# Cosine attention on one core: ten buffers for V in place of six, pair 3's squares in halves, and new engine orders

## The chip, the core and the metric

The kernel runs on one core of a Trainium2 chip. The metric is the device time of one execution in microseconds (us). The engines of the core work side by side, each through its own list of instructions in order: TensorE (PE in the profile), VectorE (DVE), ScalarE (ACT), GpSimd (POOL), and SyncE (SP), which here only issues DMA transfers. An instruction that waits for another engine holds up everything behind it on its own engine.

## The reference

Inputs Q, K, V are float32 of shape 8 x 12 x 512 x 64 (batch, heads, sequence, width), tau is 0.1. The core of it:

```python
Q_norm = Q / (np.linalg.norm(Q, axis=-1, keepdims=True) + 1e-10)
K_norm = K / (np.linalg.norm(K, axis=-1, keepdims=True) + 1e-10)
scores = np.einsum('bhqd,bhkd->bhqk', Q_norm, K_norm) / tau
weights = np.exp(scores - np.max(scores, axis=-1, keepdims=True))
weights = weights / (np.sum(weights, axis=-1, keepdims=True) + 1e-10)
return np.einsum('bhqk,bhkd->bhqd', weights, V).astype(np.float32)
```

## The kernel before, in words

The 96 heads are worked on as 48 pairs, s = 0 to 47. A pair goes through these steps, which the text names by their keys in the code:

- LD(s,0), LD(s,1), LV(s): SyncE loads Q, K and V of the pair, 256 KB each (L299, L302). For pair 0 the loads are in halves, K's on ScalarE's queue (L296).
- SQ(s): squares of Q and K, on GpSimd as one instruction (L325); for the pairs in `SQ_ON` in parts, on ScalarE or GpSimd (L317, L319); for pair 0 L227 and L229.
- SSQ(s,1), RED(s,w): sums of squares over the width. For K (and for the first pairs Q as well) TensorE adds eight slices (L342) and DVE reduces the rest (L349); otherwise DVE reduces alone (L353).
- NEW(g,k): the reciprocal norms of a group g of one to four pairs, by Newton steps on DVE (L377 to L386); for the first four pairs by a logarithm and an exponential on ScalarE, LOG(g) at L367 and NEW(g,7) at L370.
- SCL(s,w): Q and K times the reciprocal norms (L404), Q's on DVE, K's mostly on GpSimd.
- TR(s,w): TensorE transposes both (L410; pair 0 L254, L256), and EVA(s) copies the result out on DVE (L417; pair 0 L267).
- SCO(s,c): for each of four blocks c of keys, two score products on TensorE (L446), and EXP(s,c) on ScalarE (L469): exp of scores over tau for both heads, 128 x 1024. For pair 0 the first two blocks come by head, in halves of 128 x 512.
- VC(s): GpSimd copies V to bfloat16 (L474), beside a column of ones that is set once (L180).
- PV(s,h,i): the products with V on TensorE (L486), which give the sum of weights in a 65th column; RCP and NRM on DVE divide by it (L497, L499), and ST(s) stores the pair from SyncE (L503). The last pair is done in three pieces (L460, L514, L525, L527).

The scores are cosines over 0.1 and need no maximum subtracted.

Nothing is scheduled at run time: `ORDER` holds, for each engine, the numbers of the operations in the order in which they are issued. Waits are derived from what each operation needs. TensorE's list also has filler products (`-256` is one of 256 columns, L188), behind eight warm-up products (L185). Buffers are rings, whose sizes are `RINGS`:

```python
R_QK, R_V, R_SQ, R_QN, R_QT, R_ET, R_O, R_X = RINGS
```

A load into a ring waits until the buffer's last user is done. For V this is

```python
P.add(("LV", s), "sp", "ld", s + VLAG, [key("VC", s - R_V)],
      lambda e: e.dma_start(out=vf[iv][:, :, :], in_=src(V, s)), slot=f"v{iv}")
```

so LV(s) waits for VC(s - 6). SyncE's list from pair 12 on goes ST(s-12), LV(s-3), LD(s,0), LD(s,1), with small shifts.

Of the kernel before, what the change touches and what calls it, by code (L numbers as in the profile page):

```python
# [106 lines left out]
def bass_cosine_similarity_attention_kernel(  # L107
# [20 lines left out]
    qk = [sb(f"qk{i}", [128, 2, 2, NT * DIM], f32) for i in range(R_QK)]  # L128
# [156 lines left out]
    def pair(s):  # L285
# [6 lines left out]
        for w, x in ((0, Q), (1, K)):  # L292
            if s == 0:
                for h in range(2):
                    P.add(("LD", 0, w, h), "act" if w else "sp", "ldh", -1000 + h,  [],
                          lambda e, w=w, x=x, h=h: e.dma_start(out=qk[iq][:, w, h], in_=src(x, s)[:, h]), slot=f"head{w}_{h}")  # L296
                continue
            P.add(("LD", s, w), "sp", "ld1" if s == 1 else "ld", s, [*([("SCL", 0, w, 0), ("SCL", 0, w, 1), ("SQ", 0, w, 0), ("SQ", 0, w, 1)] if s == R_QK else [key("SCL", s - R_QK, w), *(squares(s - R_QK, w) if s >= R_QK else [])])],
                  lambda e, w=w, x=x: e.dma_start(out=qk[iq][:, w], in_=src(x, s)),  # L299
                  slot=f"first{s}_{w}" if s <= 2 else f"qk{iq}")  # L300
# [242 lines left out]
SQ_ON = {1: ("act", ("act", "pool")), 2: ("act", "pool")}  # L543
# [8 lines left out]
RINGS = 18, 6, 6, 3, 3, 3, 8, 3  # L552
# [17 lines left out]
def slack(s, most):  # L570
# [5 lines left out]
        "7 8 64 65 103 104 11 141 142 66 178 179 105 221 222 143 255 256 180 297 298 223 331 332 257 374 375 299 408 "  # L576
        "409 333 450 451 63 376 102 410 140 452 177 220 484 485 526 527 560 561 486 603 604 528 637 638 254 562 679 680 "
        "296 605 713 714 330 639 755 756 373 681 789 790 407 715 832 833 449 757 866 867 483 791 900 901 525 834 934 "
        "935 559 868 977 978 602 902 1011 1012 636 936 1045 1046 678 979 1079 1080 712 1013 1121 1122 754 1047 1155 "
        "1156 788 1081 1189 1190 831 1123 1223 1224 865 1157 1266 1267 899 1191 1300 1301 933 1225 1334 1335 976 1268 "  # L580
        "1368 1369 1010 1302 1411 1412 1044 1336 1445 1446 1078 1370 1479 1480 1120 1413 1513 1514 1154 1447 1555 1556 "
        "1188 1481 1589 1590 1222 1515 1623 1624 1265 1557 1657 1658 1299 1591 1699 1700 1333 1625 1733 1734 1367 1659 "
        "1767 1768 1410 1701 1444 1735 1478 1769 1512 1554 1588 1622 1656 1698 1732 1766 1796 1810 "
    ),
    "pool": (
        "0 1 2 14 27 22 35 69 4 107 50 144 89 181 224 164 127 258 207 300 230 334 377 272 360 306 241 411 283 453 349 "
        "470 394 317 436 487 529 425 459 563 606 640 501 546 535 682 512 716 578 758 792 589 835 654 688 623 869 665 "
        "903 730 699 764 741 775 937 980 807 1014 963 852 818 875 1048 909 1082 886 1124 920 952 986 1158 1020 1192 997 "
        "1226 1269 1141 1107 1031 1303 1096 1065 1175 1252 1209 1130 1337 1164 1371 1198 1320 1414 1354 1448 1241 1286 "
        "1397 1309 1482 1516 1431 1558 1343 1499 1465 1386 1420 1454 1626 1592 1660 1702 1609 1643 1736 1685 1530 1564 "  # L590
        "1598 1541 1719 1632 1575 1770 1753 1789 1674 1708 1742 1776 "
    ),
    "dve": (
        "5 13 15 26 28 19 24 21 32 71 73 37 34 109 78 111 76 80 116 114 148 146 118 151 153 182 155 184 225 227 55 185 "
        "56 186 61 187 62 188 189 94 190 95 192 191 193 194 196 100 261 101 198 259 301 303 228 262 138 263 139 264 232 "
        "265 132 266 133 267 337 268 175 269 270 169 378 170 304 274 176 380 335 212 338 213 339 218 340 219 341 342 "
        "308 343 344 345 246 347 414 247 346 252 381 253 454 351 412 288 456 383 415 294 289 416 295 417 385 418 488 "
        "419 490 420 322 422 421 323 423 328 457 329 427 530 365 532 366 491 371 492 372 493 564 494 461 607 399 495 "
        "566 496 400 498 497 405 499 406 641 503 533 609 441 567 442 568 447 569 448 570 537 571 683 572 643 574 573 "
        "475 575 576 481 476 482 717 610 580 612 685 517 644 759 645 518 646 523 614 647 524 648 793 649 551 651 719 "  # L600
        "650 552 652 557 836 558 656 686 594 761 795 720 595 721 690 722 723 870 724 600 725 838 601 727 726 628 872 "
        "629 728 904 634 635 732 762 906 670 796 671 797 676 798 677 799 766 800 938 801 802 803 805 839 704 940 710 "
        "705 711 804 809 841 981 1015 746 983 747 752 843 753 873 780 1017 781 907 1049 877 786 787 1051 823 941 942 "
        "824 943 1083 944 911 945 829 946 830 948 947 1125 950 1085 857 858 949 863 864 954 1054 984 1159 897 898 891 "
        "1127 892 988 1052 1018 1193 931 925 1161 926 932 1022 1227 1270 1195 968 1086 969 1087 974 1088 975 1089 1090 "
        "1056 1091 1093 1092 1128 1002 1229 1003 1094 1008 1009 1098 1304 1036 1272 1037 1042 1043 1162 1132 1196 1076 "
        "1077 1070 1306 1071 1338 1166 1372 1340 1230 1112 1231 1118 1113 1232 1119 1233 1200 1234 1235 1415 1237 1236 "
        "1238 1239 1146 1152 1374 1153 1147 1275 1273 1243 1341 1180 1417 1181 1307 1186 1187 1277 1449 1214 1451 1215 "
        "1483 1517 1311 1220 1221 1559 1485 1257 1375 1258 1376 1377 1378 1263 1379 1264 1380 1382 1381 1345 1452 1384 "
        "1519 1291 1292 1297 1298 1418 1388 1486 1325 1561 1326 1383 1331 1332 1422 1627 1488 1593 1359 1595 1360 1365 "  # L610
        "1366 1456 1703 1629 1402 1520 1403 1521 1522 1408 1523 1409 1524 1490 1525 1526 1527 1528 1562 1436 1663 1437 "
        "1442 1443 1532 1661 1470 1705 1471 1596 1566 1476 1477 1630 1504 1739 1505 1737 1600 1510 1511 1771 1546 1773 "
        "1547 1664 1665 1666 1667 1668 1552 1669 1553 1671 1670 1634 1672 1580 1706 1581 1586 1587 1740 1676 1774 1614 "
        "1620 1615 1621 1710 1648 1654 1649 1655 1744 1690 1691 1778 1696 1697 1724 1725 1730 1731 1758 1759 1764 1765 "
        "1801 1802 1794 1795 1808 1809 "
    ),
    "pe": (
        "6 -256 -256 -256 -256 -256 -192 23 20 -256 70 36 -256 72 -128 42 33 38 108 39 43 110 46 79 77 48 81 83 147 145 "
        "117 115 85 51 52 57 87 58 53 59 152 119 154 54 183 121 60 226 123 125 90 91 92 93 156 96 97 98 158 99 260 160 "
        "195 197 162 134 135 136 199 137 302 128 201 129 231 130 203 229 131 171 205 172 173 174 336 233 165 166 167 "  # L620
        "168 235 271 237 273 208 209 239 210 211 379 275 214 215 216 277 217 305 307 279 242 243 244 281 245 413 248 "
        "309 249 250 251 311 348 284 285 313 286 287 350 315 290 291 455 352 292 293 354 382 384 356 318 319 324 358 "
        "320 321 489 386 325 326 388 327 361 390 424 426 362 392 363 364 531 428 367 368 369 370 430 460 458 432 395 "
        "396 397 398 434 401 565 462 402 403 404 464 437 438 439 466 500 440 502 468 608 443 444 504 445 446 534 506 "
        "536 471 472 508 473 474 642 510 477 478 538 479 480 540 577 513 514 542 515 519 579 544 520 516 684 581 521 "
        "611 583 522 613 585 547 548 549 587 550 718 553 615 554 555 556 617 794 590 591 619 653 655 621 592 593 760 "
        "657 689 687 659 596 597 598 624 661 599 837 625 663 626 627 871 691 630 631 632 693 666 633 667 695 729 731 "
        "668 697 669 672 905 733 673 674 675 765 735 763 737 700 701 702 739 703 939 706 767 707 708 709 769 806 771 "
        "808 742 773 748 743 744 745 810 749 982 750 812 751 842 840 814 776 777 778 816 779 1016 782 844 783 784 876 "
        "846 874 785 819 820 848 821 822 1050 850 910 908 878 825 826 827 880 853 828 854 882 855 856 884 1084 859 912 "  # L630
        "860 861 862 914 951 953 916 887 888 889 918 893 894 895 890 955 896 1126 957 985 987 959 927 928 929 961 930 "
        "921 922 923 989 924 1160 991 1019 1021 993 964 965 970 995 966 967 1194 1023 971 972 973 1025 1055 1053 1027 "
        "998 999 1004 1029 1000 1001 1228 1057 1005 1006 1007 1059 1097 1032 1033 1061 1095 1034 1035 1063 1038 1271 "
# [60 lines left out]
```

## Time and profile before

| | |
|---|---|
| median of 4 runs | 191.08 us (190.92 to 192.71) |
| the profiled execution: its own time | 192.71 us |
| its span, first to last instruction | 190.7 us |
| busy: ACT, PE, DVE, POOL | 182.7, 177.5, 164.6, 154.9 us |
| moved by DMA | 50.75 MB, 266 GB/s over the span |
| GpSimd waiting for K loads at L325 | 5.8 us, 8 times |
| SyncE waiting at V loads (L302) for V copies (L474) | 23.9 us, 14 times |
| SyncE waiting at stores (L503) for NRM (L499) | 38.6 us, 23 times |

The times are medians over executions; the profile is of one execution, whose own time lies 2.0 us above its span. In profile rows, the first number of a timeline row is the start in us from the span's start, the second the duration; "x4" is a count of merged instructions, and the brackets give the idle time of the engine just before and what ended it. In a row of the groups, the numbers after the first bar are busy us and mean ns of one, after the second bar the idle us before them. Records of ScalarE start before the previous one has ended, so busy time there includes some waiting.

### The profile page before, as it was taken

The numbers are of one execution on the slowest core, as the hardware profiler recorded it, in microseconds if no ns is written. First come the engines' busy times: TensorE is split into PE (matmuls) and PEld (weight loads), VectorE is DVE, ScalarE is ACT, GpSimd is POOL, SyncE is SP. The second block draws the span as 40 slices with busy tenths as digits, with TensorE's granted clock in tenths as the row PEclk, the third lists the DMA queues.
The fourth block names the chain that finished last, engine by engine and source line by source line (L and its number), as shares of the span: only waits on it lengthen the run. The fifth ranks groups of instructions, "written<-read, shape, count | busy, mean of one in ns | idle before, by whom it ended". The sixth has DMA issues, their size and how long they took to land.

```text
span 190.7 us, 6683 instructions
## 1 busy us (share of the span) xinstructions
PE 177.5 (93%) x2729; PEld 110.7 (58%) x2729; DVE 164.6 (86%) x530; ACT 182.7 (96%) x214; POOL 154.9 (81%) x144
## 2 busy tenths in 40 slices
PE   7989899999999999999999999899999999999983
PEld 2636566656665566566566566555656656555552
DVE  2689999999999999999998898999898989885543
ACT  4699999999999999999999999999999999999993
POOL 3689899999999999999996998999798699260000
PEclk9999999999999999999999999999999999999999
DMA  5999996999999989999999299997899775231133
GB/s 157 343 353 349 348 359 206 314 348 373 378 344 284 286 251 311 347 322 311 327 305 335 89 281 321 344 381 257 281 274 315 255 229 155 70 112 55 58 110 110
DMA packets 52445, 50.75 MB, mean 266 GB/s; under 512 B 3136, under 2 KB 52416, under 8 KB 52416
## 3 DMA queue, kind: packets, MB, share of 16 engines
q1 hardware_dynamic: 51984, 50.02, 81.1%
q8 instruction: 21, 0.34, 0.7%
q10 hardware_dynamic: 432, 0.33, 0.5%
q14 instruction: 8, 0.07, 0.1%
HBM read 37.75 MB, written 12.58 MB: 264 GB/s over the span
## 4 chain that ended last, share of the span: by engine, by line
ACT 84%; DMA 6%; POOL 4%; PE 3%; SPq 1%; issue 1%; DVE 1%
ACT et L469 82%; DMA qk<-in_K_dram 3%; DMA qk<-in_Q_dram 3%; POOL sq L325 2%; PE scps L446 1%; POOL qn L404 1%; PE ops L342 1%; POOL vb L474 1%; PE tps L410 1%; PE ops L486 0%; SPq L296 0%; ACT et L460 0%; DVE ob L527 0%; ACT sq L317 0%; SPq L299 0%
## 5 line engine op out<-in xcount | busy, mean ns | idle before, releaser
L469 ACT ACTIVATE et<-scps 128x1024 bf16<-128x1024 f32 (+1 forms) x193 | 176.1, 1202 | 0.6 <-PE scps L446 0.5
L325 POOL TENSOR_TENSOR sq<-qk 128x1024 bf16<-128x1024 f32 x45 | 84.8, 1893 | 5.8 <-DMA qk<-in_K_dram 5.8
L446 PE MATMUL scps<-qt 64*128 64x512 bf16 x384 | 75.6, 386 | 7.0 <-ACT et L469 2.2
L486 PE MATMUL ops<-vb,et 128*128 128x65 bf16 x1504 | 75.9, 195 | 0.4 <-DVE ob L499 0.2
L486 PEld LDWEIGHTS ops<-vb,et 128*128 128x128 bf16 x1504 | 56.5, 98 | 30.5 <-issue 23.3
L404 POOL TENSOR_TENSOR qn<-qk,rk 128x512 bf16<-128x512 f32 x37 | 38.2, 1043 | 4.2 <-DVE rk L382 4.0
L499 DVE TENSOR_TENSOR ob<-ops,rd 128x256 f32<-128x256 f32 x94 | 38.8, 419 | 0.8
L404 DVE TENSOR_TENSOR qn<-qk,nps 128x512 bf16<-128x512 f32 x57 | 37.8, 677 | 0.1
L417 DVE COPY qt<-tps 128x1024 bf16<-128x1024 bf16 x47 | 32.2, 686 | 3.8 <-PE tps L410 3.5
L446 PEld LDWEIGHTS scps<-qt 64*128 64x128 bf16 x384 | 19.3, 93 | 26.0 <-ACT et L469 12.6
L410 PE MATMUL tps<-ident,qn 128*128 128x128 bf16 x376 | 33.5, 221 | 0.9 <-POOL qn L404 0.7
L353 DVE TENSOR_REDUCE nps<-sq 128x8 f32<-128x512 bf16 x44 | 29.9, 684 | 3.0 <-POOL sq L325 2.7
L474 POOL TENSOR_SCALAR vb<-vf 128x512 bf16<-128x512 f32 x48 | 29.4, 626 | 0.8 <-DMA vf<-in_V_dram 0.8
L410 PEld LDWEIGHTS tps<-ident,qn 128*128 128x128 bf16 x376 | 21.5, 98 | 12.2 <-issue 5.6
L497 DVE RECIPROCAL rd<-ops 128x4 f32<-128x4 f32 x94 | 16.3, 176 | 8.5 <-PE ops L486 6.9
L342 PE MATMUL ops<-sq,ident 128*128 128x64 bf16 x400 | 19.8, 194 | 0.3
L342 PEld LDWEIGHTS ops<-sq,ident 128*128 128x128 bf16 x400 | 14.9, 98 | 2.9 <-issue 2.0
L349 DVE TENSOR_REDUCE nps<-ops 128x8 f32<-128x64 f32 x44 | 9.3, 213 | 0.2
L377 DVE TENSOR_TENSOR nps<-nps,ys 128x32 f32<-128x32 f32 (+1 forms) x30 | 6.2, 207 | 0.2
L378 DVE SCALAR_TENSOR_TENSOR nps<-nps,ys 128x32 f32<-128x32 f32 (+1 forms) x30 | 6.2, 208 | 0.1
L185 PE MATMUL ops<-warm_in,ident 128*128 128x512 bf16 x8 | 3.6, 631 | 1.4 <-POOL eps L178 1.4
L382 DVE SCALAR_TENSOR_TENSOR nps<-nps,ys 128x16 f32<-128x16 f32 (+1 forms) x22 | 3.9, 182 | 0.1
(50 smaller groups left out, 41.0 us busy)
## 6 DMA issues: line engine op xcount, KB each, us to landing
vf<-in_V_dram SPq DMA_DIRECT2D x48, 256.0 KB, 5.4
qk<-in_Q_dram SPq DMA_DIRECT2D x47, 256.0 KB, 4.6
qk<-in_K_dram SPq DMA_DIRECT2D x47, 256.0 KB, 5.5
out_dram<-ob SPq DMA_DIRECT2D x47, 256.0 KB, 4.2
qk<-in_Q_dram SPq DMA_DIRECT2D x2, 128.0 KB, 2.7
qk<-in_K_dram ACTq DMA_DIRECT2D x2, 128.0 KB, 2.9
out_dram<-ob SPq DMA_DIRECT2D x1, 128.0 KB, 1.7
out_dram<-ob ACTq DMA_DIRECT2D x1, 64.0 KB, 1.6
```

The source lines that it names most:

```text
L325: lambda e: e.tensor_tensor(out=sqf, in0=data, in1=data, op=ALU.mult))
L342: last = e.matmul(out=o_ps[bank][:, 320:384], lhsT=ident[:, :], rhs=sq[iqs][:, 8 * w : 8 * w + 8, 8 * k : 8 * k + 8], start=(k == 0), stop ...
L353: lambda e, w=w, dst=dst: e.tensor_reduce(out=dst, in_=sq[iqs][:, 8 * w : 8 * w + 8, :], axis=AX.X, op=ALU.add))
L404: lambda e, w=w, r=r: e.tensor_tensor(out=qn[iqn][:, w].rearrange("p t h d -> p h t d"), in0=qk[iq][:, w].rearrange("p h (t d) -> p h t d" ...
L410: last = e.transpose(t_ps[:, w, t, :], qn[iqn][:, w, t].rearrange("p h d -> p (h d)"), ident[:, :])
L417: lambda e: e.tensor_copy(out=qt[iqt][:, :, :, :].rearrange("p w t x -> p (w t x)"), in_=t_ps[:, :, :, :].rearrange("p w t x -> p (w t x)")))
L446: last = e.matmul(out=sc_ps[:, 2 * b + h, :], lhsT=qt[iqt][64 * h : 64 * h + 64, 1, c, :], rhs=qt[iqt][64 * h : 64 * h + 64, 0, :, :], sta ...
L469: lambda e, c=c, b=b, hs=hs: e.activation(out=et[iet][:, c, hs[0] : hs[-1] + 1, :], in_=sc_ps[:, 2 * b + hs[0] : 2 * b + hs[-1] + 1, :], f ...
L474: lambda e: e.tensor_scalar(out=vb[:, iq, :, :, 0:DIM].rearrange("p c h d -> p h c d"), in0=vf[iv][:, :, :].rearrange("p h (c d) -> p h c ...
L486: last = e.matmul(out=o_ps[h][:, 65 * t : 65 * t + 65], lhsT=et[iet][:, c, h, 128 * t : 128 * t + 128], rhs=vb[:, iq, c, h, :], start=(c = ...
L497: lambda e, h=h, grid=grid: e.reciprocal(out=rd[io][:, h, :], in_=grid[:, :, DIM]))
L499: lambda e, h=h, grid=grid: e.tensor_tensor(out=ob[io][:, h], in0=grid[:, :, 0:DIM], in1=rd[io][:, h, :].unsqueeze(2).to_broadcast([128, N ...
```

## The change

`RINGS` gives V ten buffers in place of six. The squares of pair 3 are two GpSimd instructions, one for Q and one for K, in place of one, and its two loads get a semaphore each, so that the first half can start with Q alone. The five orders come from a new search; the numbers above 144 shift by one since pair 3 has one operation more.

```diff
-                  slot=f"first{s}_{w}" if s <= 2 else f"qk{iq}")
+                  slot=f"first{s}_{w}" if s <= 3 else f"qk{iq}")
...
-SQ_ON = {1: ("act", ("act", "pool")), 2: ("act", "pool")}
+SQ_ON = {1: ("act", ("act", "pool")), 2: ("act", "pool"), 3: ("pool", "pool")}
...
-RINGS = 18, 6, 6, 3, 3, 3, 8, 3
+RINGS = 18, 10, 6, 3, 3, 3, 8, 3
```

The orders, read back into keys. SyncE's is the same. ScalarE's differs in the first pairs only:

```
ACT before: ... SQ2.0 LOG1 EXP0.1.0 NEW1 EXP0.0.0 EXP0.0.1 EXP0.1.1 LOG2 EXP0.2 NEW2 EXP0.3 EXP1.0 EXP1.1 LOG3 NEW3 EXP1.2 ...
ACT after:  ... SQ2.0 EXP0.1.0 LOG1 NEW1 EXP0.0.0 EXP0.0.1 EXP0.1.1 LOG2 EXP0.2 NEW2 EXP0.3 EXP1.0 LOG3 EXP1.1 NEW3 EXP1.2 ...
```

TensorE's and GpSimd's starts (f is a filler with its columns; vone is the memset of L180, one, eye and eps are the constants of L174, L175 and L178):

```
PE before: warm f256 x5 f192 TR0.1.0 TR0.0.0 f256 SSQ1.0 TR0.1.1 f256 SSQ1.1 f128 SCO0.1.0 TR0.0.1 SCO0.0.0 SSQ2.0 ...
PE after:  warm f256 x3 f192 TR0.1.0 TR0.0.0 f256 SSQ1.0 TR0.1.1 f128 SCO0.1.0 SSQ1.1 TR0.0.1 SCO0.0.0 SSQ2.0 ...

POOL before: one eye eps SQ0.1.0 SQ0.1.1 SCL0.1.0 SCL0.1.1 SQ1.1.1 vone SQ2.1 VC0 SQ3.0 VC1 SQ4.0 ...
POOL after:  eps one eye vone SQ0.1.0 SQ0.1.1 SCL0.1.0 SCL0.1.1 SQ1.1.1 SQ2.1 VC0 SQ3.0 SQ3.1 VC1 SQ4.0 ...
```

and a stretch of GpSimd's in mid-run:

```
POOL before: ... SQ29 VC23 SCL24.1 SCL25.1 SQ30 SCL26.1 SQ31 VC25 SQ32 SQ33 VC29 VC28 VC26 SQ34 SCL28.1 VC27 VC30 VC32 VC31 SCL29.1 SQ35 SCL30.1 SQ36 SCL31.1 VC34 ...
POOL after:  ... SQ29 VC27 SCL24.1 SQ30 SCL25.1 VC24 SCL26.1 VC28 VC25 VC26 SQ31 SQ32 SQ33 SQ34 SCL28.1 SCL29.1 VC31 SCL30.1 SQ35 VC29 SQ36 VC32 VC34 VC30 SCL31.1 VC33 ...
```

On TensorE and DVE the operations of neighbouring pairs change places throughout.

## The prediction

> **What bounds the kernel now.** I read the page first, then ScalarE's own timeline at the start, then the chain in order of time, and last the queues of GpSimd and SyncE at the place where the chain leaves ScalarE.
>
> ```profile
> span 190.7 us, 6683 instructions
> ...
> PE 177.5 (93%) x2729; PEld 110.7 (58%) x2729; DVE 164.6 (86%) x530; ACT 182.7 (96%) x214; POOL 154.9 (81%) x144
> ...
> ACT 84%; DMA 6%; POOL 4%; PE 3%; SPq 1%; issue 1%; DVE 1%
> ...
> L469 ACT ACTIVATE et<-scps 128x1024 bf16<-128x1024 f32 (+1 forms) x193 | 176.1, 1202 | 0.6 <-PE scps L446 0.5
> L325 POOL TENSOR_TENSOR sq<-qk 128x1024 bf16<-128x1024 f32 x45 | 84.8, 1893 | 5.8 <-DMA qk<-in_K_dram 5.8
> ```
>
> ScalarE's exponentials are the bound: 193 of them, and only 0.6 us of idle before them in the whole run. The 1202 ns is no price, because the records overlap. The chain in order of time gives the price:
>
> ```profile
> 15.87 88.02 ACT et L469 x96
> ...
> 121.11 65.19 ACT et L469 x71
> ```
>
> 96 exponentials in 88.02 us are 0.917 us each, and the 71 later ones, 0.918. Between the two pieces lies a loss that the busy share hides: of 193, 175 are in the chain's other ACT pieces or ahead of it (two halves at 9.21 and 9.79), so 18 lie between. From 103.89 (end of the 96) to 122.13 (end of the first of the 71: 121.11 + 1.02) 19 exponentials end; at 0.917 that is 17.42 us, and it took 18.24. So **0.82 us** is lost in mid-run, and nowhere else after 16 us. The rest of the span is the start (first exponential at 9.21) and the end (last exponential ends at about 187.3, then 3.4 us of products, scaling and stores). Only start, middle and end can give anything.
>
> **The start.** The first exponential, and what stands ahead of it:
>
> ```profile
> 8.15 0.63 ACT L317 ACTIVATE sq<-qk 128x512 bf16<-128x512 f32 x1 [0.24 <-DMA qk<-in_Q_dram]
> 8.99 0.31 ACT L367 ACTIVATE ys<-xs,eps 128x16 f32<-128x16 f32 x1 [0.21 <-DVE xs L349]
> 9.21 0.58 ACT L469 ACTIVATE et<-scps 128x512 bf16<-128x512 f32 x1
> 9.68 0.18 ACT L370 ACTIVATE nps<-ys 128x16 f32<-128x16 f32 x1
> ```
>
> ```profile
> 7.68 0.39 PE L254 MATMUL scps<-ident,qn 128*128 128x128 bf16 x4
> 7.90 0.27 PE L188 MATMUL scps<-warm_in,ident 128*128 128x256 bf16 x1
> 8.30 0.39 PE L342 MATMUL ops<-sq,ident 128*128 128x64 bf16 x8
> 8.53 0.22 PE L188 MATMUL scps<-warm_in,ident 128*128 128x128 bf16 x1
> 8.68 0.39 PE L446 MATMUL scps<-qt 64*128 64x512 bf16 x1
> ```
>
> SSQ(1,1) (8.30) waits for a square of pair 1, made from the K load that lands late; the first score product stands behind it though its own operands (EVA, copied by 7.58) are ready. The new PE order puts the product first, after the 128-column filler: filler from about 8.05, product at about 8.2. On ScalarE the square of pair 2 (8.15 to 8.78) still stands ahead, so the first exponential starts at about 8.7 in place of 9.21: 0.5 us earlier. It then goes back. LOG(1) now comes behind that exponential. SSQ(1,1) follows the product at about 8.5 and RED 0.43 later (8.30 to 8.73 in the rows), done by 9.15; LOG(1) 9.2 to 9.5, NEW(1) 9.53 to 9.73 (9.86 before), the next exponential about 0.15 earlier than before. The scale, transpose and copy of pair 1 (L404, L410, L417) keep their order, hence also about 0.2 earlier. LOG(3) moves ahead of EXP(1,1), and everything on ScalarE queues behind that wait: it needs RED(3,1), behind pair 2's scale products on DVE. The squares of pair 3 in halves start at about 10.6 with Q and end at 12.7 (13.06 before), so RED(3,1) ends at about 14.4 where EXP(1,0) lets ScalarE go at about 14.25: 0.1 us back. Net of the start: **0.1 us gained** (ends: 0.3 lost if LOG(3) waits for a late K, 0.5 gained if nothing comes back).
>
> The split itself: two 128x512 squares at 1.04 (POOL's row of that shape) against one of 1.89 are 0.19 us more on POOL, covered by the 0.59 us it idled before that square. [...] POOL is full from 30 to 100 us, by which the split would cost 0.19; at 11 us the row shows it waiting, so it costs 0. The memset of `vb` (0.74) goes into POOL's 2.2 us wait for the first K load and frees 0.7 us at 8.1, which the K load of pair 2 uses up.
>
> Fewer fillers: three of 256 columns leave, two of them ahead of the first transposes. [...] Without the two fillers (0.21 each) TensorE idles about 0.4 us before 6.16, after some 4.3 us of unbroken work. [...] I take 0 and keep +1.0 for the range.
>
> **The middle.** Why ScalarE lost 0.82 us:
>
> ```profile
> 103.17 0.38 SPq L503 DMA_DIRECT2D out_dram<-ob  x1
> 107.42 0.37 SPq L302 DMA_DIRECT2D vf<-in_V_dram  x1
> 107.83 0.47 SPq L299 DMA_DIRECT2D qk<-in_Q_dram  x1
> 108.35 0.47 SPq L299 DMA_DIRECT2D qk<-in_K_dram  x1
> ```
>
> ```profile
> 117.40 1.89 POOL L325 TENSOR_TENSOR sq<-qk 128x1024 bf16<-128x1024 f32 x1 [0.91 <-DMA qk<-in_K_dram]
> 119.25 1.04 POOL L404 TENSOR_TENSOR qn<-qk,rk 128x512 bf16<-128x512 f32 x1
> ```
>
> SyncE is one queue. At 103.55 it stops at V of pair 32, whose buffer is free only when POOL has copied V of pair 26 (107.40, an old copy placed late), and the Q and K loads behind it wait with it. In all SyncE stands 23.9 us, 14 times, at V loads for these copies. The K loads then come late: POOL idles 5.8 us, and here 0.91 at 117.40; the scale product behind it ends at 120.29, the transpose on PE waits 0.52 for it, the score product stands behind that, and ScalarE starts at 121.11 after 0.45 of shown idle. The two smaller losses (108.5, 111.4) hang on the square at 103.74, which had waited 0.76 for K.
>
> With ten buffers V of pair 32 asks for the copy of pair 22, made long before. SyncE's order is unchanged, so it then stands only at stores (38.6 us for NRM): after the store at 103.17 the loads go at 103.6 to 104.5, **about 4 us earlier**, more than the 0.91 and 0.76 missed. POOL is next to be late only on its own work. So up to 0.82 us goes. The bytes and the count of transfers stay.
>
> **The sum.** Of the profiled run: 190.7 - 0.1 - 0.8 = 189.8 span, and with the 2.0 around it 191.8 against 192.71. But the other three runs are 190.92 to 191.17, 1.6 us under the profiled one, so they cannot hold all of its late loads. I take half of the 0.82: 191.08 - 0.1 - 0.4 = **190.6 us**. The end's order is the same on ScalarE and nearly so on PE: 0. The searched orders of PE, DVE and POOL move hundreds of instructions; by the rows no instruction gets dearer from its neighbours (all 45 whole squares on POOL take 1.89), and PE's longest burst between two score products in mid-run falls or stays, so I cost them at 0 while ScalarE covers them.
>
> **Rivals.**
> *Nothing to gain* (191.1): the unprofiled runs have no mid-run loss and LOG(3) takes the start back. For it: their 1.6 us. Against: the 23.9 us of SyncE are the program's.
> *Everything gained* (189.9): 0.82 in every run and 0.4 at the start. For it: the queue's wait is fixed by POOL's order. Against: under 189.17 it would also need the end.
> *A V load takes the place of the K load, slower* (192.0): POOL's new order puts V copies ahead of scale products, such as V of pair 34 ahead of SCL(31,1), where before it stood behind. That load was issued at 112.85 and V takes 5.4 to land: 118.3, while POOL now arrives at about 117.7. The price is known: 0.91 of waiting cost ScalarE 0.56, so a wait decides from about 0.35 on. Three such places at 0.4 give +1.2 and a slower result. Against: earlier issue by SyncE also serves V.
> [...]
>
> **How the numbers follow.** Forecast (190.2 to 190.9) 0.50, nothing gained 0.20, everything 0.13, slower by waits or clock 0.17. Range 189.4 to 192.2. 1% (1.9 us), about what a measurement of this kernel can tell from no change, is more than all of the start and middle together: faster by it 0.04, taken from the third case's edge. Slower by it needs twice the last rival's price: 0.08. The rest is within.
>
> **What would show it.** Right: no V load waiting on SyncE for POOL in mid-run; POOL's waits for K fall from 5.8 to 2 or less; exponentials of 0.917 without a break after 16 us; first exponential near 8.7, but EXP(1,2) only 0.1 to 0.3 before its 15.80. Wrong: POOL waiting for V, DVE or PE waiting for POOL's scale products with a break on ScalarE, or 128-column transposes still at 0.107 us pitch after 7.5 us.

## The result, and the profile after

The changed kernel takes 191.14 us (median of 43 runs, 190.56 to 194.56). The kernel before, run beside it, takes 191.87 us (64 runs, 190.76 to 195.74). The ratio is 0.9964 [0.9952, 0.9976]; of 191.87 that is 0.69 us less [0.46, 0.92]. Medians and quartiles here are of all runs, while the ratios leave out the slow ones, such as 3 of these 43 (193.65 to 194.56, at a mean granted TensorE clock of 0.977 to 0.986), so a ratio is not exactly the quotient of two medians. The gain is not a plain shift: the lower quartile goes from 191.33 to 190.95, the upper from 192.53 to 191.43. So the lower edge of the times moves by 0.4 us and the upper by 1.1.

The profiled execution took 190.94 us and its span is 188.9. The page of the profile, at the rows that were shown of before:

```profile
span 188.9 us, 6679 instructions
...
PE 176.4 (93%) x2726; PEld 110.3 (58%) x2726; DVE 164.9 (87%) x530; ACT 182.2 (96%) x214; POOL 154.8 (82%) x145
...
ACT 94%; DMA 3%; SPq 1%; issue 1%; DVE 1%; PE 0%
...
L469 ACT ACTIVATE et<-scps 128x1024 bf16<-128x1024 f32 (+1 forms) x193 | 175.8, 1243 | 0.0
L325 POOL TENSOR_TENSOR sq<-qk 128x1024 bf16<-128x1024 f32 x44 | 82.8, 1893 | 3.0 <-DMA qk<-in_K_dram 2.9
```

The chain is on ScalarE for 94% of the span instead of 84%; POOL, 4% before, is gone from it, and PE's share falls from 3% to 0. The chain in order of time (start, length, what) says this most sharply:

```profile
14.93 169.58 ACT et L469 x185
```

From 14.93 us to 184.51 ScalarE runs 185 exponentials without a break, 0.917 each. The 169.57 us are a ruler for all that follows: in the eight other kernels below whose trace has no break, the same 185 take 169.54 to 169.59 us. Such a kernel differs from another almost only by when the 185 begin.

ScalarE's timeline at the start:

```profile
7.48 0.63 ACT L317 ACTIVATE sq<-qk 128x512 bf16<-128x512 f32 x1 [0.31 <-DMA qk<-in_Q_dram]
8.04 0.60 ACT L469 ACTIVATE et<-scps 128x512 bf16<-128x512 f32 x1
8.64 0.31 ACT L367 ACTIVATE ys<-xs,eps 128x16 f32<-128x16 f32 x1
8.98 0.19 ACT L370 ACTIVATE nps<-ys 128x16 f32<-128x16 f32 x1
9.10 1.56 ACT L469 ACTIVATE et<-scps 128x512 bf16<-128x512 f32 x3
...
13.63 0.31 ACT L367 ACTIVATE ys<-xs,eps 128x16 f32<-128x16 f32 x1
13.85 1.00 ACT L469 ACTIVATE et<-scps 128x1024 bf16<-128x1024 f32 x1
14.75 0.18 ACT L370 ACTIVATE nps<-ys 128x16 f32<-128x16 f32 x1
14.86 3.75 ACT L469 ACTIVATE et<-scps 128x1024 bf16<-128x1024 f32 x4
```

and, of before, the rows up to EXP(1,2):

```profile
15.33 0.32 ACT L367 ACTIVATE ys<-xs,eps 128x16 f32<-128x16 f32 x1
15.68 0.19 ACT L370 ACTIVATE nps<-ys 128x16 f32<-128x16 f32 x1
15.80 3.75 ACT L469 ACTIVATE et<-scps 128x1024 bf16<-128x1024 f32 x4
```

A zero of time must be set first. The square of pair 2 waits for its Q load and begins at 7.48, against 8.15 before. Nothing shows that these 0.67 us are the change's: the loads stand in the same order, and below the square begins anywhere from 7.48 to 8.52 with the new start and from 7.75 to 8.28 with the old. Counted from this square, the first exponential begins after 0.56 us (8.04 - 7.48) instead of 1.06 (9.21 - 8.15), and EXP(1,2) after 7.38 (14.86 - 7.48) instead of 7.65 (15.80 - 8.15). The new order is worth 0.27 us in this pair of traces.

So the two spans differ by 1.8 us like this: 0.67 a load that landed earlier, 0.27 the order of the start, 0.86 the breaks in mid-run (before needs 186.30 - 15.87 = 170.43 us for the 185, 0.86 over the ruler; the prediction reckoned 0.82); together 1.80.

TensorE's timeline at the start shows the fillers left out, and the score product (L446) moved ahead of the adding products of SSQ(1,1) (L342, 7.94):

```profile
6.13 0.52 PE L256 MATMUL scps<-ident,qn 128*64 128x128 bf16 x4 [0.30 <-POOL qn L246]
...
7.25 0.38 PE L254 MATMUL scps<-ident,qn 128*128 128x128 bf16 x4
7.47 0.22 PE L188 MATMUL scps<-warm_in,ident 128*128 128x128 bf16 x1
7.62 0.39 PE L446 MATMUL scps<-qt 64*128 64x512 bf16 x1
7.94 0.41 PE L342 MATMUL ops<-sq,ident 128*128 128x64 bf16 x8
```

and, of before, the first transposes:

```profile
6.16 0.64 PE L256 MATMUL scps<-ident,qn 128*64 128x128 bf16 x4
```

In mid-run the waits of SyncE and of GpSimd (us in total, times, longest) were:

```profile
SPq L503 <- DVE ob L499: 45.4, 25, 3.5
...
SPq L302 <- POOL vb L474: 4.0, 6, 1.1
```

```profile
POOL sq L325 <- DMA qk<-in_K_dram: 2.9, 6, 1.1
```

The 23.9 us at V loads have become 4.0 (and another 2.0, three times, that the trace puts down to a scale product in front of the copy). SyncE now stands at stores instead: 45.4 for 38.6 behind NRM. Over everything that it is shown waiting for, V loads go from 25.4 to 7.5 us and stores from 58.8 to 77.0: the 18 us are not saved but spent at the stores. What its stop did to the loads is seen in the stretches 100 to 112 us, where the last two columns are the DMA share and GB/s. First before, then after:

```profile
104.00:108.00 4.00, 3.58 (x56) 2.19 (x56) 2.67 (x12) 4.00 (x5) 4.00 (x5) 1.00 0.35 118
108.00:112.00 4.00, 3.85 (x66) 2.53 (x64) 3.88 (x13) 3.93 (x5) 4.00 (x5) 1.00 0.73 249
```

```profile
104.00:108.00 4.00, 3.66 (x51) 2.09 (x52) 3.97 (x16) 4.00 (x5) 3.77 (x3) 1.00 1.01 339
108.00:112.00 4.00, 3.92 (x65) 2.55 (x64) 3.15 (x9) 4.00 (x6) 4.00 (x5) 1.00 0.93 299
```

Before, with SyncE stopped from 103.55 to 107.42, the DMA engines were busy for a third of the time (118 GB/s); the K load was late at 117.40. After, they are busy for 1.01 and 0.93 of these stretches (339 and 299 GB/s).

### The profile page after: what moved, and what is told of

Its sections match the earlier page's. It is cut to its first block, busy times and chain, and to the rows that moved or that the text cites. A ratio compares the mean times of both kernels' runs of the same rounds, so it can differ in the third digit from the quotient of the medians.

```text
span 188.9 us, 6679 instructions
## 1 busy us (share of the span) xinstructions
PE 176.4 (93%) x2726; PEld 110.3 (58%) x2726; DVE 164.9 (87%) x530; ACT 182.2 (96%) x214; POOL 154.8 (82%) x145
## 4 chain that ended last, share of the span: by engine, by line
ACT 94%; DMA 3%; SPq 1%; issue 1%; DVE 1%; PE 0%
ACT et L469 92%; DMA qk<-in_Q_dram 3%; SPq L299 0%; SPq L296 0%; ACT et L460 0%; ACT ys L367 0%; DVE ob L527 0%; ACT sq L317 0%; ACT nps L370 0%; PE ops L514 0%; DVE rd L525 0%
## 5 line engine op out<-in xcount | busy, mean ns | idle before, releaser
L325 POOL TENSOR_TENSOR sq<-qk 128x1024 bf16<-128x1024 f32 x44 | 82.8, 1893 | 3.0 <-DMA qk<-in_K_dram 2.9
L446 PE MATMUL scps<-qt 64*128 64x512 bf16 x384 | 75.6, 386 | 7.3 <-ACT et L469 2.0
L486 PE MATMUL ops<-vb,et 128*128 128x65 bf16 x1504 | 74.5, 195 | 0.0
L486 PEld LDWEIGHTS ops<-vb,et 128*128 128x128 bf16 x1504 | 56.1, 98 | 27.8 <-issue 21.5
L499 DVE TENSOR_TENSOR ob<-ops,rd 128x256 f32<-128x256 f32 x94 | 39.3, 419 | 0.9
L446 PEld LDWEIGHTS scps<-qt 64*128 64x128 bf16 x384 | 19.5, 92 | 26.1 <-ACT et L469 9.8
L342 PE MATMUL ops<-sq,ident 128*128 128x64 bf16 x400 | 20.0, 194 | 0.0
L342 PEld LDWEIGHTS ops<-sq,ident 128*128 128x128 bf16 x400 | 15.0, 98 | 4.1 <-issue 2.7
L319 POOL TENSOR_TENSOR sq<-qk 128x512 bf16<-128x512 f32 (+1 forms) x4 | 3.7, 932 | 0.9 <-DMA qk<-in_K_dram 0.9
```

The costliest lines, as they stand in the source:

```text
L325: lambda e: e.tensor_tensor(out=sqf, in0=data, in1=data, op=ALU.mult))
L342: last = e.matmul(out=o_ps[bank][:, 320:384], lhsT=ident[:, :], rhs=sq[iqs][:, 8 * w : 8 * w + 8, 8 * k : 8 * k + 8], start=(k == 0), stop ...
L446: last = e.matmul(out=sc_ps[:, 2 * b + h, :], lhsT=qt[iqt][64 * h : 64 * h + 64, 1, c, :], rhs=qt[iqt][64 * h : 64 * h + 64, 0, :, :], sta ...
L486: last = e.matmul(out=o_ps[h][:, 65 * t : 65 * t + 65], lhsT=et[iet][:, c, h, 128 * t : 128 * t + 128], rhs=vb[:, iq, c, h, :], start=(c = ...
L499: lambda e, h=h, grid=grid: e.tensor_tensor(out=ob[io][:, h], in0=grid[:, :, 0:DIM], in1=rd[io][:, h, :].unsqueeze(2).to_broadcast([128, N ...
```

## The experiments

The change has three parts: the ring, the start (orders, halves, fillers), and the orders after it. The kernels were measured in three groups, and each ratio is to the kernel before, run beside the group. Its own median was 191.60 beside the first four below, 191.87 beside after_v8 and the burst, and 192.17 beside newstart_v10 and the last three. This drift is as large as the effects, so ratios are compared first, and across groups only with care.

### One part at a time

**Ring alone** (before_v10), on the kernel before:

```diff
-RINGS = 18, 6, 6, 3, 3, 3, 8, 3
+RINGS = 18, 10, 6, 3, 3, 3, 8, 3
```

> The kernel before with ten V buffers and nothing else. Theory (the ring frees SyncE's queue, so K loads come in time in mid-run): about 0.4 us under the kernel before (half to all of the 0.82 us of mid-run loss), SyncE's 23.9 us at V loads near 0, no break between exponentials after 16 us. Rival (the searched orders of mid-run carry it): equal to before, within 0.1 us, with GpSimd still waiting some 5 us for K. Rival (only the start counts): equal to before, and the queue's waits gone without effect.

Measured: 191.31 us, ratio 0.9991 [0.9974, 1.0008]. The profiled run has no break on ScalarE, and the 185 start within 0.15 us of before's 15.87:

```profile
15.72 169.59 ACT et L469 x185
```

GpSimd's waits for K are 2.7 us. Alone the ring makes no difference that this comparison resolves: from 0.50 us faster to 0.15 slower, which holds the 0.4 of the expectation and nothing as well. The quartiles lie closer, 191.17 and 191.65 (14 runs) against 191.25 and 192.22.

**Everything but the ring** (after_v6):

```diff
-RINGS = 18, 10, 6, 3, 3, 3, 8, 3
+RINGS = 18, 6, 6, 3, 3, 3, 8, 3
```

> The changed kernel with the ring put back to six. Theory of the ring: gives back about 0.4 us of the 0.7 gained, K waits on GpSimd return to 5 us. Rival of the orders: as fast as the changed kernel, since its orders were searched with late loads. Rival of the start: as fast as the changed kernel too, within 0.1 us.

Measured: 192.38 us, ratio 1.0041 [1.0019, 1.0063]: slower than before. The searched orders with six buffers cost more than the new start gives, so both rivals of the expectation fell. The trace shows a path like that of before. SyncE's waits, then the stretches (DMA share and GB/s last), GpSimd's timeline and ScalarE's:

```profile
SPq L302 <- POOL vb L474: 21.5, 11, 5.1
```

```profile
88.00:92.00 4.00, 3.95 (x70) 2.61 (x68) 3.97 (x14) 4.00 (x6) 4.00 (x5) 1.00 0.77 259
92.00:96.00 4.00, 3.89 (x67) 2.45 (x63) 3.75 (x14) 4.00 (x6) 3.41 (x4) 1.00 0.91 209
96.00:100.00 4.00, 3.98 (x69) 2.58 (x68) 3.95 (x11) 4.00 (x5) 4.00 (x6) 1.00 1.03 350
100.00:104.00 4.00, 4.00 (x72) 2.67 (x71) 3.58 (x13) 4.00 (x6) 4.00 (x4) 1.00 1.09 382
104.00:108.00 4.00, 3.52 (x53) 2.11 (x50) 3.96 (x15) 4.00 (x6) 2.32 (x2) 1.00 1.09 379
```

```profile
104.99 1.89 POOL L325 TENSOR_TENSOR sq<-qk 128x1024 bf16<-128x1024 f32 x1 [0.56 <-DMA qk<-in_K_dram]
108.06 1.89 POOL L325 TENSOR_TENSOR sq<-qk 128x1024 bf16<-128x1024 f32 x1 [1.18 <-DMA qk<-in_K_dram]
```

```profile
111.77 6.52 ACT L469 ACTIVATE et<-scps 128x1024 bf16<-128x1024 f32 x7 [1.28 <-PE scps L446]
```

At one of these stops SyncE stood from 85.9 to 89.3. The rate falls to 259 and 209 GB/s, then stays at 350 to 382 with the engines full and the loads still behind: the backlog is not worked off by 108, when K is 1.18 us late. ScalarE stands idle for 1.28 (1.39 over the ruler). Read so, a stop of the queue is paid for some 20 us after it; no run here takes out one stop alone.

**New start alone, six buffers** (newstart_v6): the kernel before with

```diff
-SQ_ON = {1: ("act", ("act", "pool")), 2: ("act", "pool")}
+SQ_ON = {1: ("act", ("act", "pool")), 2: ("act", "pool"), 3: ("pool", "pool")}
...
-                  slot=f"first{s}_{w}" if s <= 2 else f"qk{iq}")
+                  slot=f"first{s}_{w}" if s <= 3 else f"qk{iq}")
```

and the orders of after up to SCO(2,1) on TensorE, RCP(0,0) on DVE, SQ(5) on GpSimd and EXP(2,0) on ScalarE; behind these, the orders of before.

> The kernel before with the new start alone (pair 3's squares in halves and the new orders of the first three to five pairs, six V buffers, old orders from there on). Theory: 0.27 us under before, as the rows of the two starts give it when both are counted from pair 2's square on ScalarE (8.66 us to the end of EXP(1,2) before, 8.39 after). Rival of the start: the whole 0.7 us. Rival of ring and orders: 0.

Measured: 191.25 us, ratio 0.9996 [0.9973, 1.0018], that is from 0.52 us faster to 0.34 slower: the 0.27 of the expectation is inside, and so is nothing. Its lowest time, 190.32, is the lowest of all kernels and its lower quartile is 191.0, but its upper is 192.0: a lower floor with much of the old upper end. Its trace bears on the ring:

```profile
SPq L302 <- POOL vb L474: 21.9, 17, 3.4
POOL sq L325 <- DMA qk<-in_K_dram: 2.9, 7, 0.7
15.23 169.55 ACT et L469 x185
```

With six buffers SyncE stands at V loads nearly as long as before (21.9 for 23.9), at the same place too (102.87 to 105.64, 2.8 us where it was 3.9), and from 104 to 108 us the rate falls as low (113 GB/s). Yet no later K load is more than 0.24 us late up to 122, and ScalarE has no break at all. So a stop at a V load does not make a break by itself. In before, K had been late twice ahead of that stop, by 0.83 us at 101.10 and 0.76 at 103.74; here once, by 0.52 at 101.95. What makes the margin differ from one execution to the next is not shown.

It and after_v6 differ only in the orders behind the start, both with six buffers, and their intervals just part (1.0018 against 1.0019). This points to those orders for the cost of after_v6.

**Ring and later orders, old start** (oldstart_v10): after with `SQ(3)` whole and the start's orders of before.

```diff
-SQ_ON = {1: ("act", ("act", "pool")), 2: ("act", "pool"), 3: ("pool", "pool")}
+SQ_ON = {1: ("act", ("act", "pool")), 2: ("act", "pool")}
...
-                  slot=f"first{s}_{w}" if s <= 3 else f"qk{iq}")
+                  slot=f"first{s}_{w}" if s <= 2 else f"qk{iq}")
```

The orders of before stand up to the same four operations, those of after behind them.

> The changed kernel with the old start (squares of pair 3 whole, old orders of the first three to five pairs), ten V buffers and the new orders from there on. Theory: about 0.3 us over the changed kernel, so 0.4 under before. Rival of the start: as slow as before.

Measured: 191.39 us, ratio 0.9983 [0.9963, 1.0002], no break. It is level with the ring alone (191.31, same group): with ten buffers the searched orders behind the start bring nothing that can be seen.

**New start and ring, old later orders** (newstart_v10): newstart_v6 with `RINGS = 18, 10, ...`.

> The new start and ten V buffers, with the old orders from pair 3 on: all of the change but the search of the mid-run. Theory (start and ring are the gain, and the new orders of mid-run bring nothing of their own): as fast as the changed kernel within 0.15 us, 0.35% under before. Rival (the new orders carry the rest): between before and the changed kernel, like ten buffers alone (0.1% under before).

Measured: 190.93 us, ratio 0.9931 [0.9899, 0.9964], quartiles 190.72 and 191.18, no break. These two parts give all that the whole change gives (0.9964 in its own comparison); whether they give more stays open, as the intervals overlap. The kernel differs from newstart_v6 in the ring alone, and their intervals lie apart (0.9964 against 0.9973); but they are of two groups, and in plain times it is only 190.93 against 191.25.

### How many buffers

after_v8 is after with

```diff
-RINGS = 18, 10, 6, 3, 3, 3, 8, 3
+RINGS = 18, 8, 6, 3, 3, 3, 8, 3
```

> The changed kernel with eight V buffers (with six it lost 1.39 us in one break at 112 us, behind K loads late by 0.56 and 1.18). Theory: the loss comes from copies that the new GpSimd order places late, each blocking SyncE through the ring; eight buffers free two more copies, so most of the wait of SyncE at V loads goes (under 10 us from 21.5) and the time lies within 0.2 us of ten buffers, about 0.5 under before. Rival: the new orders need all ten, and eight is half-way, about equal to before.

Measured: 191.07 us, ratio 0.9952 [0.9933, 0.9972], no break; GpSimd's waits for K 1.2 us. SyncE's waits:

```profile
SPq L302 <- POOL vb L474: 4.3, 6, 2.0
```

Eight are as good as ten: 4.3 us of waiting where ten have 4.0 and six 21.5.

### A burst of late loads

Does the ring, or the new orders, carry the kernel over loads that come late from elsewhere? Three kernels get eight extra loads of 256 KB into unused buffers (their lines from L129 on are numbered one higher):

```diff
+for k in range(8):
+    P.add(("XL", k), "sp", "ld", 0, [], lambda e, k=k: e.dma_start(out=xl[k][:, :, :], in_=src(V, k)), slot=f"outx{k}")
```

SyncE issues two of them ahead of each of LD(32,0), LD(33,0), LD(34,0) and LD(35,0).

before_late is built so on before:

> The kernel before with eight more loads of 256 KB into unused buffers, two ahead of each of the Q and K loads of pairs 32 to 35: some 5.6 us of DMA work more in mid-run, nothing else. Theory: with six V buffers SyncE has no lead to absorb it, so the break in mid-run grows from 0.8 to 2 or 3 us; 1.5 us or more over before. Rival (K loads do not set mid-run): the same as before within 0.3 us.

before_v10_late on the ring alone:

> The same eight extra loads with the old orders and ten V buffers. Theory: the ring gives the lead, so at most half of the loss of the six-buffer kernel with extra loads. Rival (the new orders give the robustness): as slow as the six-buffer kernel with extra loads.

and after_late on the changed kernel:

> The changed kernel with the same eight extra loads. Theory of the ring: loses as little as the old orders with ten buffers, 0 to 0.7 us over the changed kernel. Rival of the orders: loses clearly less than the old orders with ten buffers, since they were searched with late loads. Third possibility: loses more, since the new order puts copies of V ahead of scale products.

Measured: 196.02, 195.71 and 195.94 us; ratios to the kernel before 1.0204 [1.0158, 1.0250], 1.0193 [1.0159, 1.0227] and 1.0224 [1.0182, 1.0265]. All three come out about 4 us over the kernel before, with breaks of 4.00, 4.67 and 5.71 us over the ruler in the profiled runs. Set against the same kernel without the burst, the changed one loses more, 2.6% where the other two lose 2.0%, though the intervals do not part them. My expectation that ten buffers would absorb part of the burst fell. SyncE's waits in before_v10_late suggest why:

```profile
SPq L504 <- DVE ob L500: 47.2, 21, 3.9
```

With the V waits gone, SyncE stands at the store of the pair twelve earlier, and the loads behind it lead no further than that store lets them. By this reading the ring takes away one stop and does not buy a long lead; no burst was run with a longer lead. That the searched orders would stand the burst better, the rival in the last expectation, fell too.

A second loss is on TensorE. The row of its granted clock in after_late, in 40 slices of 4.9 us:

```profile
PEclk9999999999999999999999957999999999999998
```

Behind the break it falls to 0.50 (114 to 118 us), and four transposes take 0.61 us at 113.41, where after_v6 has 0.40 at 111.01; the next breaks of ScalarE come there. The other two show such a fall as well, 0.50 from 110 to 112 us in before_late and 0.58 to 0.56 from 114 to 118 in before_v10_late, and no kernel without the burst has such a fall. How the 4 us divide between late loads and the slower TensorE is not measured.

### Would a longer lead help?

after_lead is after with each store of pairs 3 to 34 six loads later in SyncE's list:

```
SP of after: ... ST(s-12) LV(s-3) LD(s,0) LD(s,1) LV(s-2) LD(s+1,0) LD(s+1,1) ...
SP here:     ... LV(s-3) LD(s,0) LD(s,1) LV(s-2) LD(s+1,0) LD(s+1,1) ST(s-12) ...
```

> The changed kernel with each store of pairs 3 to 34 moved two groups of loads later on SyncE, so that loads run ahead by some 7 us more. SyncE stands 47 us at stores now, so loads could go earlier. Theory (no K load is late any more in the changed kernel): nothing in the median, at most 0.2 us, GpSimd's waits for K in mid-run at 0. Rival (K loads still cost in undisturbed runs): 0.3 us or more faster. It could be slower if the late stores hold up DVE through the ring of eight output buffers.

Measured: 190.99 us, ratio 0.9938 [0.9906, 0.9971], against 0.9931 of newstart_v10 in the same group. GpSimd waits 0.9 us for K, SyncE 52.1 at stores. No gain is seen over newstart_v10 with its 3.3 us of K waits, and none of the traces with eight or ten buffers has a break for such waits to cause. The changed kernel itself was not in this group (0.9964 in its own), so the rival's 0.3 us are not excluded.

### The parts of the start

**Square of pair 3 whole** (after_whole3): after with

```diff
-SQ_ON = {1: ("act", ("act", "pool")), 2: ("act", "pool"), 3: ("pool", "pool")}
+SQ_ON = {1: ("act", ("act", "pool")), 2: ("act", "pool")}
...
-                  slot=f"first{s}_{w}" if s <= 3 else f"qk{iq}")
+                  slot=f"first{s}_{w}" if s <= 2 else f"qk{iq}")
```

> The changed kernel with pair 3's squares in one instruction. Theory: the halves end the squares some 0.4 us sooner, and LOG(3) then waits for the reduction: the break ahead of LOG(3) grows from 0.04 to about 0.3 us, and the time by as much (0.15%). Rival (the logarithm has slack): no difference, within 0.1 us.

Measured: 191.72 us, ratio 0.9993 [0.9957, 1.0029]. The chain in order of time:

```profile
10.54 1.90 POOL sq L325
12.44 0.05 issue
12.49 0.41 PE ops L342 x8
12.89 0.34 PE scps L446 x2
13.23 0.02 issue
13.26 1.02 ACT et L469
...
15.47 169.58 ACT et L469 x185
```

Pair 2's square starts at 7.49 here, as in after, and the 185 start 0.54 us later (15.47, 14.93). Not all of that is the square's: the first exponential is already 0.23 late (8.27, 8.04), since TensorE's transposes of pair 0 took 0.63 us for four, twice, where after has 0.52 and 0.39. The trace of after_v6 has the halves and the same slow transposes; its first exponential starts at 8.27 and its EXP(0,3) at 12.01, both as here, and then:

```profile
15.16 77.00 ACT et L469 x84
```

So the whole square costs 0.31 us, the size that was expected. I had looked for it ahead of LOG(3). It lies elsewhere: TensorE's new order has SSQ(3,0) ahead of SCO(1,0), and with a whole square it waits for K's load and for all 1.90 us of the square while the score product stands behind. EXP(1,0) then starts at 13.26. With halves, Q's square alone frees it: in after the products of SSQ(3,0) stand at 11.67 and the score product at 12.20, here at 12.49 and 12.82.

**LOG(1) back ahead of the first exponential** (after_log1):

```
ACT of after: ... SQ2.0 EXP0.1.0 LOG1 NEW1 EXP0.0.0 ...
ACT here:     ... SQ2.0 LOG1 EXP0.1.0 NEW1 EXP0.0.0 ...
```

> The changed kernel with LOG(1) back ahead of the first exponential. Theory: ScalarE waits for RED(1,1) with nothing to do, so the first exponential starts about 0.5 us later (1.0 after pair 2's square in place of 0.55); part comes back since LOG(1) is then out of the way, and 0.3 us stay. Rival (it all comes back): no difference.

Measured: 191.34 us, ratio 0.9962 [0.9928, 0.9997]; newstart_v10 in the same group has 0.9931, and the intervals overlap. Pair 2's square starts at 8.52 and the first exponential at 9.64, 1.12 later, as in the order before. The 185 start at 16.01, 7.49 after the square; in after it is 7.45 (14.93 - 7.48). Beside that trace nearly all of the half microsecond has come back within ten exponentials, and 0.04 stays lost; beside the commonest value of the new start, 7.24 in the table below, 0.25 does. The 0.3 that I expected is at the upper end, and one profile doesn't settle it.

### Where the 185 begin

In every profiled run whose start has the old or the new orders unchanged (the kernels with a burst too, since it comes far behind the start), the 185 exponentials, or the first piece of them, start at so many us, and so long after pair 2's square:

| start | kernels: start of the 185, after pair 2's square |
|---|---|
| old | before 15.87, 7.72; before_v10 15.72, 7.65; oldstart_v10 15.43, 7.68; before_late 15.93, 7.65; before_v10_late 15.08, 7.25 |
| new | after 14.93, 7.45; newstart_v10 15.12, 7.24; after_v6 15.16, 7.57; after_v8 15.20, 7.25; newstart_v6 15.23, 7.24; after_late 15.48, 7.24 |

The means after the square are 7.59 and 7.33: by them the new start is worth 0.26 us, about what the pair of traces above gave. The commonest values, 7.65 to 7.72 and 7.24 to 7.25, lie 0.4 apart. And before_v10_late shows that the old orders reach 7.25 too, when pair 2's Q comes late (0.77 us of waiting) and holds up the start alone. The square is not a clean zero, since TensorE's work on pair 0 can be the later one: in after_v6, with 7.57, it is. So the worth of the start is 0.3 to 0.4 us in most of these traces, and no single figure. (after_lead, whose row merges the squares, starts at 14.81.)

## Why the prediction was right, and where a term was off

- **The size.** Forecast: 190.6, that is 0.48 us or 0.25% under the median shown. Measured: 0.36% [0.24, 0.48]. Sign and size hold, the gain a little above the forecast. In absolute time the kernel came out at 191.14, since the base was off: four runs gave 191.08, sixty-four give 191.87, and the lower quartile of those is 191.33. Three of the four shown lay in the lowest quarter.
- **First exponential 0.5 earlier.** Held: 0.50 from pair 2's square.
- **What goes back at the start.** Forecast 0.4, measured 0.23 in this pair of traces: this term was mis-sized, and the start gives 0.27 (up to 0.4 by the table) instead of 0.1. LOG(1) and NEW(1) behind the first exponential took nearly all of it back (the second exponential 1.62 after the square instead of 1.64, where 0.15 was forecast). What I had not counted came behind: the third exponential no longer waits 0.15 for its score product, and NEW(3) no longer follows LOG(3) directly; it moves ScalarE's end by 0.08 (14.85 to 14.93) where it took 0.22 before (15.65 to 15.87), 0.14 less. LOG(3) waited 0.04 (its piece of the chain is 0.23, LOG(2)'s 0.19), forecast 0.1.
- **Halves of pair 3.** "It costs 0" held: POOL's row after has the two halves in 2.04 us. But their worth was looked for at LOG(3), and after_whole3 beside after_v6 shows it at SSQ(3,0) on TensorE, 0.31 us.
- **Fillers.** The gap was forecast at 0.4 and is 0.30; the transposes behind it run at 0.52 for four at 6.13 (0.64 at 6.16 before) and 0.38 at 7.25. In after_lead the gap is 0.60, and the four behind it take 0.41 at once. No run shows the +1.0 us that the range kept for slower transposes at the start: the 185 begin 7.24 to 7.57 us after pair 2's square with the new start, 7.25 to 7.72 with the old, and in after_whole3, where four transposes took 0.63 twice, the first exponential is 0.23 later than in after. Nor does the pitch of 0.107 us last: before has it at 6.16 ((0.64 - 0.32) / 3, of which 0.32 is the first alone), after has 0.05 to 0.06 at 7.25 and 8.18 (0.38 and 0.39 for four, 0.22 for the first alone).
- **The 0.82 of mid-run.** In the profiled run all of it is gone, and so it is in all eight traced kernels with eight or ten buffers and no burst, before_v10 among them, which changes nothing but the ring. Of the three with six, before loses 0.86 us, after_v6 1.39 and newstart_v6 nothing. So the prediction was right that the V waits are the program's (23.9, 21.5 and 21.9 us), but the break behind them is not: before has it, newstart_v6, with the same ring and the same later orders, does not. The "half" allowed for that, but its size was a guess from three unprofiled runs and no reckoning. The total of 0.69 less the start's 0.27 to 0.4 leaves 0.3 to 0.4, so half agrees, with some luck and only as a remainder: before_v10, which measures the ring by itself, cannot tell it from nothing. The time saved is uneven, 0.4 at the lower quartile and 1.1 at the upper, which fits breaks that some executions have and others not; only the profiled executions show their breaks, so for the rest this stays an inference.
- **SyncE and K.** V waits gone but for 4.0 us of short ones; POOL's K waits 2.9, where 2 or less was the sign. The sign was too strict, and the total is not what tells: there is no break here at 2.9, nor in newstart_v10 at 3.3, and waits late in the run cost ScalarE nothing (1.44 at 151.32 in before, 1.58 at 140.41 in before_v10). Between 90 and 120 us, where the breaks lie, K waits come to 2.50 us in before and 1.74 in after_v6, which have breaks, and to 0.52 in newstart_v6 and at most 0.33 with eight or ten buffers, which have none.
- **Rivals.** *Nothing to gain* is outside the interval. *Everything gained* describes the profiled run (no break at all), not the median. *A V load takes the K load's place*: POOL waited for V once, 0.3 us, below the 0.35 from which it was to decide. In before_v10 it waited twice, one of the waits 1.5 us (at 161.58, late in the run), with no break on ScalarE, so the 0.35 is no general threshold. What I had costed at 0, the searched orders, has a price in one setting: with six buffers, 0.45% between newstart_v6 and after_v6.

What stays open: which of the moved operations of the searched orders makes them worse with six buffers; why the kernel before drifts by 0.6 us between groups; and how the 0.69 us divide between ring and start, since neither alone can be told from no change and both together can.

## What to carry to other kernels

Here the loads of three tensors in SyncE's one queue shared the stops of each. In before it stood at V from 103.55 to 107.42, Q and K behind it went at 107.83 and 108.35, and GpSimd waited 0.91 us for a K load at 117.40; in after_v6 it stood from 85.9 to 89.3, and a K load was 1.18 late at 108.06. By this reading a ring that is too short for one tensor delayed the others, and the bill came some 10 to 20 us later at ScalarE, which never touched that ring (0.86 and 1.39 us). It need not: newstart_v6 has the stops without the bill, so one trace without a break does not show that a ring is long enough. Enlarge the ring until the long waits at that load are gone from the queue's own waits (here with eight buffers), and look at the quartiles: the ring alone moved the upper one from 192.22 to 191.65 and left the lower nearly alone (191.25 to 191.17). When the bound engine runs without a break, compare kernels by when its unbroken stretch begins.

## What the runs showed that was not expected

- The unbroken stretch is the same within 0.05 us of 169.57 in nine kernels with different orders on the other engines. What is left of the spread of their spans (188.8 to 189.9) lies in the first 16 us.
- The landing of pair 2's Q moves by 1 us between executions with the same loads in the same order: its square starts at 7.48 in after and 8.52 in after_log1.
- The ScalarE group row shows 0.6 us of idle before and 0.0 after, while the breaks were 0.86 and 0.00 by the ruler: recorded idle hides part of a break, because the records overlap (a mean of 1202 ns each before, at one every 917 in the chain).
- How soon TensorE is fast at the start differs between executions of the same start: four transposes take 0.41 us at 5.73 in after_v8 and still 0.63 at 6.35 in after_whole3, with the old start 0.41 at 6.16 in before_v10 and 0.64 at 6.16 in before. The granted clock of those stretches reads 1.00 in all four, so it does not show this.
- Eight extra loads, 2.1 MB or by estimate 5.5 us at 380 GB/s (after_v6 moved 379 to 383 from 100 to 112 us), cost about 4 us with either ring. How much slack the loads had can't be read from that, as TensorE's granted clock stood at 0.50 to 0.58 for some us in all three.
